# Retention with samples: small copies moved to GpSimd, and the last head's loads asked for in another order

## The chip, the cores and the metric

The kernel runs on one core of one Trainium2 chip. Its time is the device time of a whole execution in microseconds (us), the median of several runs. The core has a tensor engine (TensorE, in the profile PE for its matmuls and PEld for its weight loads), a vector engine (VectorE, DVE), a scalar engine (ScalarE, ACT), GpSimd (POOL), and SyncE (SP), which here only issues DMAs. Each engine works through its own list of instructions strictly in order. A DMA is issued by one of them, here mostly by SyncE and some by ScalarE, and an issue that has to wait holds up everything behind it on that engine.

## The reference

One inference step of a hybrid decoder: 1024 prompt tokens, and 8 sequences of 4 new tokens each (the samples, 32 rows). All is float32. The inputs, normalised, go through one wide projection; retention with 4 heads and latent attention (MLA) with 8 heads work beside each other on its parts; both are gated, projected, merged and projected again. The change is in the retention:

```python
def retention_chunk(q, k, v, s_prev, log_g):
    ...
    scores = jnp.einsum('bihd,bjhd->bhij', q, k) * dmask[None]
    intra = jnp.einsum('bhij,bjhe->bihe', scores, v)
    q_decay = jnp.exp((idx[:, None] + 1.0) * log_g[None, :])
    cross = jnp.einsum('bihd,bhde->bihe', q, s_prev) * q_decay[None, :, :, None]
    k_decay = jnp.exp((c - 1.0 - idx)[:, None] * log_g[None, :])
    s_new = (jnp.exp(c * log_g)[None, :, None, None] * s_prev
             + jnp.einsum('bjhd,bjhe->bhde', k * k_decay[None, :, :, None], v))
    return intra + cross, s_new
```

For the prompt this runs over 8 chunks of 128 tokens with the state (256 x 512 per head) carried along. For the samples it runs once, with a state of its own for each sequence that is read from memory (state_ret) and written back (ret_sample). q and k are rotated by tables of cosines and sines before.

## The kernel before, in words

A float32 matmul that must be exact is done as three: each operand is split into a high and a low part, and the products high x high, low x high and high x low are summed in PSUM. These are lines 268 to 270; one such group is called a triple here. A column block of a projection is 8 triples deep for each third (352 tokens) of the tokens; the thirds go through two PSUM banks, named mm. The gates' columns are emptied by ScalarE (L441, tile gev, two rooms) and stored by a DMA that ScalarE issues (L444).

The retention goes head by head. For a head, head_qk projects and rotates q and k (tables cosR and sinR; the last steps of a third are L848 to L853 on VectorE and GpSimd), and copies the samples' 32 columns into the small tiles qS and kS (L869). head_w loads and splits the weights of the values. prompt_chunks then takes the 8 chunks: front makes the scores and turns k (knl is read back from memory, where SyncE stored it, L951), values_of projects the values (vnh and vnl, two rooms each, L887 on ScalarE), and back updates the state S (first chunk L972 on ScalarE, later L970 on VectorE), splits it (Sth on GpSimd, Stl on VectorE), and makes the output, which is normalised (L894 to L906), turned on VectorE (tile g) and stored (go).

sample_state follows at the end of a head. It projects the values of the 32 rows with plain weights (wvS, eight blocks of 128x512, which use the rooms of vnh and vnl, four in all; matmuls L1090), copies them (vs, ScalarE, L1098), spreads them (L1101), and then takes four pieces of the state (st, two tiles of 512 KB each; calls of states): it multiplies them with q (L1122), adds k times v (L1136, VectorE L1138) and stores them (L1140).

These parts are Python generators. A function woven() interleaves two of them by their declared costs: the last chunk's remains and the samples of a head go beside the next head's projections, and for the last head beside three columns of the MLA gate. The written order is then rearranged once more by a scheduler that works with its own estimates of when a tile's room or data is ready. So the order on each engine is fixed when the program is built, and a load that seems ready earlier can draw the work that uses it forward. With the last head, the next phase's latents (lat, krT), rope weights (wr and wqr, rope_weights, L1156 and L1158) and projections' weights are asked for on SyncE's queue too.

A room is named by a tag: tiles with the same tag share rooms, and a new tile waits for the last reader of the room's old tile.

Of the kernel before, what the change touches and what calls it, by code (L numbers as in the profile page):

```python
# [10 lines left out]
F32 = mybir.dt.float32  # L11
# [9 lines left out]
P = 128  # L21
D = 1024
SEQ = 1024
# [3 lines left out]
NT = SEQ + NR  # L27
# [4 lines left out]
HR = 4  # L32
DK = 256
DV = 512
# [10 lines left out]
C_RQ, C_RK, C_RV, C_RG, C_LAT, C_MG, C_GA, C_GB = 0, 1024, 2048, 4096, 6144, 6848, 7872, 8896  # L45
# [117 lines left out]
def decode_step(ctx: ExitStack, tc: tile.TileContext, A: dict, O: dict):  # L163
    nc = tc.nc
    pe, act, dve, pool, sp = nc.tensor, nc.scalar, nc.vector, nc.gpsimd, nc.sync
# [18 lines left out]
    def ac():  # L184
        return banks["pool"].tile([P, 512], F32, tag="ac", name="ac", bufs=3)
# [3 lines left out]
    def slots(pl, tag, bufs):  # L189

        return lambda name, shape=(P, NT), dt=F32R: pl.tile(list(shape), dt, tag=tag, name=name, bufs=bufs)
# [35 lines left out]
    w_in = A["w_in"][0]  # L227
# [223 lines left out]
    def chain(*gs):  # L451
        for g_ in gs:
            yield from g_
# [355 lines left out]
    p4 = ph.enter_context(tc.tile_pool(name="p4", bufs=1))  # L809
# [5 lines left out]
    vs = p4.tile([P, DV], F32, name="vs")  # L815
    pool.memset(vs, 0.0)
    tok = slots(p4, "tok", 4)
    cosR, sinR = (p4.tile([P, NT], F32, name=n) for n in ("cosR", "sinR"))
    sp.dma_start(cosR, A["ropeR"][:, 0, :])
    sp.dma_start(sinR, A["ropeR"][:, 1, :])  # L820
    lg = _log_g()
# [4 lines left out]
    def head_qk(h, X):  # L826
        cols = [col + h * DK + m * P for col in (C_RQ, C_RK) for m in range(2)]
        ws = []

        def ask():  # L830
            if cols:
                col = cols.pop(0)
                ws.append(load_w(w_in[:, col:col + P], 8))

        ask()
        for name in "qk":
            dst = X[name] = [tok(f"{name}{m}", dt=F32) for m in range(2)]

            def first(j, ps, sl, dst=dst):
                act.copy(dst[0][:, sl], ps)  # L840

            def second(j, ps, sl, dst=dst, name=name):
                x = wst.tile([P, TH], F32, tag="gev", name="rx", bufs=2)
                act.copy(x, ps)
                c, s = cosR[:, sl], sinR[:, sl]
                x0, x1 = dst[0][:, sl], dst[1][:, sl]
                t = [p4.tile([P, TH], F32, tag=f"rt{i}", name=f"rt{i}", bufs=1) for i in range(2)]
                dve.tensor_tensor(out=t[0], in0=x0, in1=s, op=ALU.mult)  # L848
                dve.tensor_tensor(out=x1, in0=x, in1=c, op=ALU.mult)
                pool.tensor_tensor(out=x1, in0=x1, in1=t[0], op=ALU.add)  # L850
                dve.tensor_tensor(out=t[1], in0=x, in1=s, op=ALU.mult)
                dve.tensor_tensor(out=x0, in0=x0, in1=c, op=ALU.mult)
                pool.tensor_tensor(out=x0, in0=x0, in1=t[1], op=ALU.subtract)  # L853
                if name == "k":
                    n = min(TH, SEQ - j * TH)
                    bs = slice(j * TH // 32, (j * TH + n) // 32)
                    for m in range(2):
                        st = p4.tile([P, TH], F32, tag=f"rt{m}", name="kb", bufs=1)[:, :n].rearrange("p (b r) -> p b r", r=32)
                        dve.transpose(st, dst[m][:, j * TH:j * TH + n].rearrange("p (b r) -> p b r", r=32))
                        for a in range(0, P, 32):  # L860
                            sp.dma_start(kD[h % 2][bs, :, m * P + a:m * P + a + 32].rearrange("b i f -> i b f"), st[a:a + 32])
            for m, evac in enumerate((first, second)):
                for i, cost in enumerate(gemm(ws.pop(0), xn, evac, 8)):
                    if i == 3:
                        ask()
                    yield cost
            own = X[name + "S"] = p4.tile([P, 2, NR], F32, tag=name + "S", name=name + "S", bufs=2)
            for m in range(2):
                act.copy(own[:, m], dst[m][:, SEQ:])  # L869

    def head_w(h, X):

# [56 lines left out]
    def prompt_chunks(h, X):  # L929
        q, k = X["q"], X["k"]  # L930
# [69 lines left out]
        def ahead(u):  # L1000

            for cost in u:
                if cost is None:
                    return
                yield cost
# [6 lines left out]
        due, done = iter(()), 0.0  # L1012
        for c in range(8):
            if c == 7:
                X["st"] = [states(h, 0, 0)]
            u = back(c, parts)
            if c < 7:
                if c:
                    parts = front(c + 1)
                    yield 1.0  # L1020
                coming = values_of(c + 1, X, V)
                if c < 2:
                    yield from islice(coming, 3)
                both = woven((chain(due, ahead(u)), 3.5), (coming, 9.0))
                for cost in both:
                    yield cost
                    if c == 0:
                        done += cost
                        if done > 3.5:
                            parts, done = front(1), -99.0  # L1030
                            yield 1.0
                due = u
        yield None
        yield from due
        yield from ahead(u)
        X["st"].append(states(h, 0, 1))
        yield from u
        sp.dma_start(O["ret_prompt"][0, 0, h].rearrange("(m p) e -> p m e", p=P), S.rearrange("p (m e) -> p m e", m=2))

    def states(h, i, m):  # L1040

        pairs = []
        for half in range(2):
            if h + 1 == HR and i:
                st = tok("st", (P, 2, DV), F32)
            else:
                st = p4.tile([P, 2, DV], F32, tag="st", name="st", bufs=4)
            sp.dma_start(st, A["state_ret"][0].rearrange("(r i) h (m p) e -> i m h p r e", i=2, m=2)[i, m, h][:, 2 * half:2 * half + 2])
            pairs.append(st)
        return pairs  # L1050

    def sample_state(h, X):

        q, k = X["qS"], X["kS"]
        g4 = float(np.exp(NS * lg[h]))

        def weights(k):
            raw = p4.tile([P, DV], F32, tag="vn" + "hl"[k % 2], name="wvS", bufs=2)
            sp.dma_start(raw, w_in[k * P:(k + 1) * P, C_RV + h * DV:C_RV + (h + 1) * DV])
            return raw  # L1060

        raws_ = [weights(k) for k in range(4)]
        ks = p4.tile([P, 2, 4, 4, 8], F32, tag="knh", name="ks", bufs=2)
        for m in range(2):
            pool.tensor_copy(ks[:, m], k[:, m].rearrange("p (r x) -> p r x", x=8).unsqueeze(2).to_broadcast([P, 4, 4, 8]))
# [22 lines left out]
        for n in range(8):  # L1088
            for r in range(4):
                pe.matmul(ps[r * NR:(r + 1) * NR, :P], xS[:, n], raws_[n][:, r * P:(r + 1) * P], start=n == 0, stop=n == 7,  # L1090
                          tile_position=(0, r * NR), skip_group_check=True)
            if n < 4:
                raws_.append(weights(n + 4))
            if n == 3:
                yield 4.0
        for r in range(4):
# [21 lines left out]
        for n, (i, m) in enumerate(turns):  # L1118
            pairs = loaded.pop(0)
            st = [pairs[r // 2][:, r % 2, :] for r in range(4)]  # L1120
            for r in range(4):
                ins = pe.matmul(px[32 * r:32 * r + 32, :], qm[:, m, r, i], st[r], start=False, stop=n == 3,  # L1122
                                tile_position=(0, 32 * r), skip_group_check=True)
                if n > 1:
                    tc.keep_in_program_order(ins)
            if n == 3:
                on = group_norm(px, P, C("qdS", h, 1), C("qd2S", h, 1))
                if h + 1 < HR:
                    late.append((h, on, NS * 2, SEQ))
                else:  # L1130
                    turn_out(h, on, NS * 2, SEQ, (wst, "wl", 2))
                    store_out(sp)
            pd = [ac(), ac(), tr(), tr()]
            for r in range(4):
                rs = slice(32 * r, 32 * r + 32)
                pe.matmul(pd[r], kxs[i][rs, m * P:(m + 1) * P], vst[rs], start=True, stop=True, tile_position=(32 * r, 0))  # L1136
            for r in range(4):
                dve.scalar_tensor_tensor(out=st[r], in0=st[r], scalar=g4, in1=pd[r], op0=ALU.mult, op1=ALU.add)  # L1138
                if r % 2:
                    sp.dma_start(out[i, m, h][:, r - 1:r + 1], pairs[r // 2])  # L1140
            if n < 2:
                loaded.append(states(h, *turns[n + 2]))
            yield 3.8

# [20 lines left out]
    X, first_w = {}, []  # L1165
    run(head_in(0, X))
    for h in range(HR):
# [7 lines left out]
        else:  # L1175
            raws = [(qkA if i < 3 else qkB)("lat", (P, SEQ), F32) for i in range(5)]
# [12 lines left out]
        X = nxt  # L1189
# [245 lines left out]
    for h in range(HM):  # L1435
        ahead = prep(h + 1) if h + 1 < HM else iter(())
# [288 lines left out]
    raws = []  # L1725
# [110 lines left out]
```

## Time and profile before

| | us |
|---|---|
| timed runs: median (lowest to highest of three) | 2119.05 (2117.35 to 2122.88) |
| profiled execution: span | 2129.5 |
| TensorE busy in it | 2079.5 |
| VectorE, ScalarE, GpSimd busy | 1237.4, 692.8, 305.4 |

No time of the profiled execution other than its span is given; it is 10.5 us above the median of the timed runs. The retention lies from about 700 to 1330 us of that span. In the profile, a line that lists an instruction ends with the idle time of its engine before it, and with what ended that idle time. Matmuls overlap, so the start of one to the start of the next is their pace, not the duration. The list of waits of one engine gives the total, the number and the longest.

### The profile page before, as it was taken

What the parts mean: (1) busy time and instruction counts of PE and PEld (TensorE: products, weight loads), DVE (VectorE), ACT (ScalarE), POOL (GpSimd) and SP (SyncE); (2) the same over time, 40 slices, a digit from 0 to 9 for tenths busy, and PEclk for the clock granted to TensorE, in tenths of its full rate; (3) what the DMA queues carried; (4) which work ended last, traced back from release to release, by engine and by line L of the source; (5) the groups of instructions that cost most, each with busy time, mean ns of one, the idle gap of its engine ahead of it and who ended that gap; (6) DMA issues with size and microseconds to landing.
All of it is one profiled execution on the core that took longest, in us unless ns stands there. A gap on an engine that the chain in (4) does not pass through costs nothing. (4 is left out here: it accounts for less than half of the span.)

```text
span 2129.5 us, 38253 instructions
## 1 busy us (share of the span) xinstructions
PE 2079.5 (98%) x15122; PEld 1792.7 (84%) x15122; DVE 1237.4 (58%) x2699; ACT 692.8 (33%) x1455; POOL 305.4 (14%) x517
## 2 busy tenths in 40 slices
PE   8999999999999999999999999999999999999998
PEld 7898777777777897888878786788888999999976
DVE  6524555465655357667676663877777465454443
ACT  6312222433333222222222221454556232232221
POOL 2210110111110022222222120122211000000000
PEclk9999999999999999999999999999999999999999
DMA  7576656566565332554634746210112565236642
GB/s 211 129 241 211 234 186 237 187 244 216 211 228 178 111 94 51 175 163 120 204 67 151 191 134 221 64 49 18 38 52 92 187 217 173 89 122 132 172 153 91
DMA packets 387188, 321.90 MB, mean 151 GB/s; under 512 B 197984, under 2 KB 332320, under 8 KB 382912
## 3 DMA queue, kind: packets, MB, share of 16 engines
q1 hardware_dynamic: 290816, 205.86, 33.0%
q0 software_dynamic: 9216, 83.89, 10.5%
q10 hardware_dynamic: 86976, 29.70, 5.2%
q8 instruction: 119, 1.95, 0.4%
q14 instruction: 61, 0.50, 0.1%
HBM read 246.69 MB, written 72.69 MB: 150 GB/s over the span
## 5 line engine op out<-in xcount | busy, mean ns | idle before, releaser
L268 PE MATMUL mm<-xh,wh 128*128 128x352 f32 x1344 | 456.5, 340 | 4.8 <-ACT gev L441 3.2
L270 PE MATMUL mm<-xh,wl 128*128 128x352 f32 x1344 | 437.0, 325 | 2.1 <-DVE wl L200 2.1
L269 PE MATMUL mm<-xl,wh 128*128 128x352 f32 x1344 | 436.7, 325 | 0.0
L268 PEld LDWEIGHTS mm<-xh,wh 128*128 128x128 f32 x1344 | 253.7, 189 | 88.5 <-issue 76.8
L270 PEld LDWEIGHTS mm<-xh,wl 128*128 128x128 f32 x1344 | 254.6, 189 | 2.9 <-DVE wl L200 2.4
L269 PEld LDWEIGHTS mm<-xl,wh 128*128 128x128 f32 x1344 | 254.7, 189 | 2.5 <-issue 1.3
L691 DVE STREAM_TRANSPOSE kt<-craw 128x512 f32<-128x512 f32 x256 | 161.3, 681 | 108.8 <-PE sc L695 75.4
L200 DVE TENSOR_TENSOR wl<-wr,wh 128x512 fp32r<-128x512 f32 (+2 forms) x203 | 136.9, 686 | 98.7 <-ACT wh L249 69.1
L249 ACT CAST wh<-wr 128x512 fp32r<-128x512 f32 x150 | 89.8, 617 | 196.5 <-PE mm L269 169.8
L441 ACT ACTIVATE gev<-mm 128x352 f32<-128x352 f32 x120 | 55.5, 462 | 230.4 <-PE mm L270 221.8
L268 PE MATMUL mm<-mh,wh 128*128 128x352 f32 x384 | 124.8, 325 | 2.2 <-ACT mh L1210 0.8
L269 PE MATMUL mm<-ml,wh 128*128 128x352 f32 x384 | 124.7, 325 | 0.8 <-DVE ml L200 0.6
L270 PE MATMUL mm<-gh,wl 128*128 128x352 f32 x384 | 124.3, 324 | 0.0
L268 PE MATMUL mm<-gh,wh 128*128 128x352 f32 x384 | 124.3, 324 | 0.0
L270 PE MATMUL mm<-mh,wl 128*128 128x352 f32 x384 | 124.2, 324 | 0.0
L269 PE MATMUL mm<-gl,wh 128*128 128x352 f32 x384 | 124.1, 323 | 0.0
L268 PE MATMUL mm<-wv,xh 128*128 128x512 f32 x256 | 101.7, 397 | 0.0
L270 PE MATMUL mm<-wv,xl 128*128 128x512 f32 x256 | 100.9, 394 | 0.0
L269 PE MATMUL mm<-wv,xh 128*128 128x512 f32 x256 | 100.8, 394 | 0.0
L695 PE MATMUL sc<-kt,q 32*32 32x512 f32 x2560 | 91.2, 600 | 0.0
L268 PEld LDWEIGHTS mm<-mh,wh 128*128 128x128 f32 x384 | 72.4, 189 | 3.2 <-ACT gh L1210 1.2
L269 PEld LDWEIGHTS mm<-ml,wh 128*128 128x128 f32 x384 | 72.3, 188 | 1.6 <-DVE ml L200 1.4
(416 smaller groups left out, 4292.3 us busy)
## 6 DMA issues: line engine op xcount, KB each, us to landing
wr<-in_w_in_dram SPq DMA_DIRECT2D x144, 256.0 KB, 3.5
st<-in_state_ret_dram SPq DMA_DIRECT2D x32, 512.0 KB, 5.7
out_ret_sample_dram<-st SPq DMA_DIRECT2D x32, 512.0 KB, 3.1
gt<-gev ACTq DMA_DIRECT2D x48, 176.0 KB, 2.1
gl<-go SPq DMA_DIRECT2D x16, 528.0 KB, 5.1
rg<-gt SPq DMA_DIRECT2D x16, 528.0 KB, 4.2
gate<-ga SPq DMA_DIRECT2D x16, 528.0 KB, 3.6
wvS<-in_w_in_dram SPq DMA_DIRECT2D x32, 256.0 KB, 4.6
```

Of the source, the lines that this page charges most:

```text
L200: dve.tensor_tensor(out=out, in0=src, in1=b32(hi), op=ALU.subtract)
L249: hi_by[0](hi, raw)
L268: pe.matmul(out, wh, xh, start=first, stop=False)
L269: pe.matmul(out, wh, xl, start=False, stop=False)
L270: pe.matmul(out, wl, xh, start=False, stop=last)
L441: a = act.activation(t, ps, func)
L691: dve.transpose(kt[:, 2 * i + s].rearrange("p (n r) -> p n r", r=32), src)
L695: pe.matmul(sc[32 * v:32 * v + 32, q, :], Q["q4"][qs_, j + v // 2, 2 * (g % 2) + v % 2, :], kt[qs_, v, :], start=n == 0, stop=n == NJ // 2 ...
```

## The change

It has three parts. The samples' copies of q and k are made by GpSimd instead of ScalarE, for all four heads. In the last head, the value weights of the samples no longer all use the rooms of vnh and vnl: four of the eight go, two by two, into the rooms of the tables cosR and sinR, which no later head needs, and are asked for before the sixth chunk; two more are asked for after the last full chunk and two after the last chunk's matmuls. And the last two pieces of the state are asked for ahead of the last chunk's output stores, instead of within sample_state. For the last head the remains of the seventh chunk (its turn and store) come after the matmuls of the eighth.

```diff
-    cosR, sinR = (p4.tile([P, NT], F32, name=n) for n in ("cosR", "sinR"))
+    cosR, sinR = (p4.tile([P, NT], F32, tag=n, name=n) for n in ("cosR", "sinR"))
...
-                act.copy(own[:, m], dst[m][:, SEQ:])
+                pool.tensor_copy(own[:, m], dst[m][:, SEQ:])
...
+            if h + 1 == HR and c == 5:
+                X["raws"] = [raw for n in range(2) for raw in two_weights(h, 2 * n, ("cosR", "sinR")[n])]
             u = back(c, parts)
...
                 due = u
+        if h + 1 == HR:
+            X["raws"].extend(sample_weights(h, k) for k in (4, 5))
         yield None
-        yield from due
-        yield from ahead(u)
+        if h + 1 < HR:
+            yield from due
+            yield from ahead(u)
+        else:
+            yield from ahead(u)
+            X["raws"].extend(sample_weights(h, k) for k in (6, 7))
+            yield from due
         X["st"].append(states(h, 0, 1))
+        if h + 1 == HR:
+            X["st"].extend(states(h, 1, m) for m in range(2))
         yield from u
...
+    def sample_weights(h, k):
+        raw = p4.tile([P, DV], F32, tag="vn" + "hl"[k % 2], name="wvS", bufs=2)
+        sp.dma_start(raw, w_in[k * P:(k + 1) * P, C_RV + h * DV:C_RV + (h + 1) * DV])
+        return raw
+
+    def two_weights(h, k, tag):
+        raw = p4.tile([P, 2, DV], F32, tag=tag, name="wvS2")
+        sp.dma_start(raw, w_in[k * P:(k + 2) * P, C_RV + h * DV:C_RV + (h + 1) * DV].rearrange("(s p) e -> p s e", p=P))
+        return [raw[:, i, :] for i in range(2)]
...
-        raws_ = [weights(k) for k in range(4)]
+        raws_ = X["raws"] if h + 1 == HR else [sample_weights(h, k) for k in range(4)]
...
-            if n < 4:
-                raws_.append(weights(n + 4))
+            if len(raws_) < 8:
+                raws_.append(sample_weights(h, n + 4))
...
-            if n < 2:
+            if n < 2 and h + 1 < HR:
                 loaded.append(states(h, *turns[n + 2]))
```

The orders on three engines show what this moves. First SyncE's queue from the last head's latents on, before (st is a piece of the state, go the outputs, krT and lat the latents):

```order
L1048 DMA st<-in_state_ret_dram 128x2x512 x2
L1178 DMA lat<-latD 128x1024
L1181 DMA krT<-latD 64x1024 x2
L924 DMA go_105<-g 32x16x32 x4
L1048 DMA st<-in_state_ret_dram 128x2x512 x2
L924 DMA go_105<-g 32x16x32 x4
L1038 DMA out_ret_prompt_dram<-S 128x2x512
L1059 DMA wvS<-in_w_in_dram 128x512 x8
L1156 DMA wr<-in_w_uq_dram 128x4x64 x3
L1048 DMA st<-in_state_ret_dram 128x2x512 x2
```

and the same stretch in the changed kernel, where line numbers after the edit are higher by up to 15 (1059 is st there, 1065 wvS, 1155 the state's store, 1171 the rope weights):

```order
L1193 DMA lat<-latD 128x1024 x2
L1196 DMA krT<-latD 64x1024 x2
L1065 DMA wvS<-in_w_in_dram 128x512 x2
L924 DMA go_105<-g 32x16x32 x4
L1059 DMA st<-in_state_ret_dram 128x2x512 x4
L924 DMA go_105<-g 32x16x32 x4
L1049 DMA out_ret_prompt_dram<-S 128x2x512
L1155 DMA out_ret_sample_dram<-st 128x2x512 x2
L1171 DMA wr<-in_w_uq_dram 128x4x64 x3
L1155 DMA out_ret_sample_dram<-st 128x2x512 x2
```

The weights' last two stand ahead of both groups of output stores, the states between them, and the rope weights behind the first two stores of a state. The other six blocks are further up the queue: four of them, as two DMAs, around the last k's store, some rows after the tables' last use.

Second TensorE, at the samples of the last head, before:

```order
L270 MATMUL mm<-xh_127,wl 128x352
L1090 MATMUL ac<-wvS,xS 32x128 x32
L1101 MATMUL tr<-vs,turn 128x512
L1114 MATMUL ac<-vs,sms 128x512
L1122 MATMUL ac<-st,qm 32x512 x5
L1136 MATMUL ac<-vst,kx 128x512 x2
```

and now (gate triples stand at the dots: 8, 5, 4):

```order
L1105 MATMUL ac<-wvS_13290,xS 32x128 x8
L1105 MATMUL ac<-wvS_13292,xS 32x128 x8
...
L1105 MATMUL ac<-wvS,xS 32x128 x16
...
L1116 MATMUL tr<-vs,turn 128x512
...
L1129 MATMUL ac<-vs,sms 128x512
L1137 MATMUL ac<-st,qm 32x512 x4
L1151 MATMUL ac<-vst,kx 128x512 x2
```

Before, 40 gate triples stood ahead of the first of these and 24 behind; now 8 stand ahead of the first sixteen, 8 ahead of the next sixteen, and the others between the later steps.

Third GpSimd, at the last head's first chunk, before:

```order
L850 TENSOR_TENSOR k_12432<-k_12432,rt_12750 128x352
L900 TENSOR_TENSOR gr<-gv,cst 128x1
L853 TENSOR_TENSOR k_12431<-k_12431,rt_12751 128x352
L197 TENSOR_SCALAR Sth<-S 128x512 x4
```

and now:

```order
L850 TENSOR_TENSOR k_12432<-k_12432,rt_12750 128x352
L869 COPY kS<-k_12432 128x32
L900 TENSOR_TENSOR gr<-gv,cst 128x1
L853 TENSOR_TENSOR k_12431<-k_12431,rt_12751 128x352
L869 COPY kS<-k_12431 128x32
L197 TENSOR_SCALAR Sth<-S 128x512 x4
```

Each copy stands right behind the instruction that makes its input, and the second one ahead of the split of the state. On ScalarE the same copies are gone, and nothing else moved there until the gates' columns of the last head.

More of the change, by code (lines that the diff above doesn't have):

```diff
@@ L1055, in sample_state @@
         g4 = float(np.exp(NS * lg[h]))
[L1057 to L1060, printed above, removed]
-        raws_ = [weights(k) for k in range(4)]
+        raws_ = X["raws"] if h + 1 == HR else [sample_weights(h, k) for k in range(4)]
         ks = p4.tile([P, 2, 4, 4, 8], F32, tag="knh", name="ks", bufs=2)
```

## The prediction

> **What bounds the kernel now.** I read the busy table first, then the list of waits of TensorE, then the windows around the last retention head, and last the engines' instructions in order of time there.
>
> ```profile
> span 2129.5 us, 38253 instructions
> PE 2079.5 (98%) x15122; PEld 1792.7 (84%) x15122; DVE 1237.4 (58%) x2699; ACT 692.8 (33%) x1455; POOL 305.4 (14%) x517
> ```
>
> TensorE (PE) is busy for all but 2129.5 - 2079.5 = 50.0 us. The change adds and removes no matmul, so it can only win back waits of PE, and time in which PE counts as busy but runs below its pace. From PE's list of waits, the three that the change is about:
>
> ```profile
> PE ac L269 <- DVE vnl L200: 4.5, 7, 1.0
> PE ac L1090 <- DMA wvS<-in_w_in_dram: 3.5, 3, 2.1
> PE tr L1101 <- ACT vs L1098: 1.2, 1, 1.2
> ```
>
> The columns are the total in us, how often, and the longest. The last two are one place, the end of the last head. Windows there (length, then busy time of PE, PEld, DVE, ACT, POOL, the granted PE clock, the DMA share and GB/s):
>
> ```profile
> 1276.10:1296.30 20.20, 20.20 (x128) 19.97 (x125) 4.03 (x12) 4.02 (x8) 1.81 (x6) 1.00 0.77 213
> 1296.30:1312.90 16.60, 11.93 (x92) 3.85 (x91) 3.78 (x8) 2.97 (x9) 0.51 (x1) 0.69 0.62 193
> 1312.90:1330.30 17.40, 17.40 (x100) 12.91 (x98) 10.31 (x20) 1.60 (x3) 0.56 (x1) 1.00 0.71 264
> 1330.30:1340.00 9.70, 7.66 (x35) 6.32 (x34) 8.15 (x20) 6.89 (x15) 2.09 (x4) 0.82 0.44 107
> ```
>
> From 1296.3 to 1312.9 PE idles for 4.7 us, and its clock stands at 0.69 on average: the busy 11.9 us are slow ones. What runs there, PE in order of time (start, duration, line):
>
> ```profile
> 1276.70 0.41 PE L268 MATMUL mm<-xh,wh 128*128 128x352 f32 x1
> ...
> 1296.31 1.08 PE L1090 MATMUL ac<-wvS,xS 128*32 128x128 f32 x32
> 1299.46 0.43 PE L1090 MATMUL ac<-wvS,xS 128*32 128x128 f32 x8 [2.07 <-DMA wvS<-in_w_in_dram]
> ...
> 1301.96 1.30 PE L1090 MATMUL ac<-wvS,xS 128*32 128x128 f32 x16 [1.20 <-DMA wvS<-in_w_in_dram]
> 1304.44 2.08 PE L1101 MATMUL tr<-vs,turn 128*128 128x512 f32 x2 [1.18 <-ACT vs L1098]
> 1306.31 1.91 PE L1114 MATMUL ac<-vs,sms 128*128 128x512 f32 x2
> ...
> 1312.89 0.43 PE L268 MATMUL mm<-xh,wh 128*128 128x352 f32 x1
> ...
> 1322.50 1.06 PE L1122 MATMUL ac<-st,qm 128*32 128x512 f32 x8
> ...
> 1323.93 0.43 PE L268 MATMUL mm<-xh,wh 128*128 128x352 f32 x1
> ...
> 1331.81 0.36 PE L268 MATMUL ac<-wqr,lh 128*128 128x256 f32 x1 [1.31 <-ACT lh L1224]
> ```
>
> PE has used up 40 gate triples (L268 to L270) by 1296.31 and then has only the samples' chain, whose value weights (wvS) are not there: a DMA, PE, a ScalarE (ACT) copy, PE, one after the other with nothing between. The weights are late because of SyncE's queue:
>
> ```profile
> 1276.99 4.63 SPq L924 DMA_DIRECT2D go<-g  x4
> 1288.03 10.55 SPq L1059 DMA_DIRECT2D wvS<-in_w_in_dram  x8
> ```
>
> Their first DMA is issued at 1288.03, behind the output stores (go), and the eight take 10.55 us, since only four rooms exist.
>
> **The last head, part by part.** The order lists put the sixteen matmuls of the first four weights 8 gate triples after the start of this stretch, the other sixteen 8 later, and the rest of the chain with 5, 4, 9, 6, 2, 9 and 13 triples between its steps. The total is 64 triples in both kernels. So the price of the new stretch is its work at full pace. The pace comes from the head before, where the same chain ran among other matmuls:
>
> ```profile
> 1149.57 1.08 PE L1090 MATMUL ac<-wvS,xS 128*32 128x128 f32 x32
> 1150.58 0.43 PE L268 MATMUL mm<-xh,wh 128*128 128x352 f32 x1
> ...
> 1161.60 1.02 PE L1101 MATMUL tr<-vs,turn 128*128 128x512 f32 x2
> ...
> 1162.62 0.32 PE L269 MATMUL mm<-xl,wh 128*128 128x352 f32 x1
> ...
> 1164.88 1.02 PE L1114 MATMUL ac<-vs,sms 128*128 128x512 f32 x2
> ...
> 1167.54 0.32 PE L269 MATMUL mm<-xl,wh 128*128 128x352 f32 x1
> ```
>
> Gate triples: (1296.31 - 1276.70) / 40 = 0.490 us each, 64 of them 31.4. L1090: 1150.58 - 1149.57 = 1.01 for sixteen, 2.0 for both. L1101: up to the second matmul of the next triple, less one third of a triple, 1162.62 - 1161.60 - 0.16 = 0.9. L1114 with the first state: 1167.54 - 1164.88 - 0.16 = 2.5. The other three states: 1323.93 - 1322.50 = 1.43 each, 4.3. Sum 41.1 us. Today the stretch lasts from 1276.70 to the end of the gates, 1331.81 - 1.31 = 1330.50: 53.8 us. The difference is **12.7 us**. Of it 3.5 + 1.2 = 4.7 are waits; at most 0.31 x 16.6 = 5.1 is the clock; the rest is the state matmuls that today go one by one at VectorE's (DVE's) pace.
>
> Whether new waits eat it, step by step from 1276.70. The first four weights go into the tables of cosines and sines, asked for when those are dead, some 70 us ahead. The last pair is asked for after the final chunk's matmuls, ahead of the 4.63 us of stores, near 1273 instead of 1288. PE wants it at 1276.70 + 16 x 0.49 + 1.0 = 1285.5. What could delay it is the traffic:
>
> ```profile
> 1260.00:1270.00 10.00, 10.00 (x46) 8.00 (x45) 6.70 (x19) 1.55 (x3) 3.09 (x8) 1.00 0.98 305
> mg<-gev ACTq DMA_DIRECT2D x9, 176.0 KB, 4.3
> wr<-in_w_uq_dram SPq DMA_DIRECT2D x3, 128.0 KB, 4.4
> L1138 DVE SCALAR_TENSOR_TENSOR st<-st,ac 128x512 f32<-128x512 f32 x32 | 20.7, 675 | 7.0 <-PE tr L1136 6.4 <-PE ac L1136 0.6
> ```
>
> The DMA engines are full there. Four weights of 256 KB are added, 1 MB at 305 GB/s: 3.4 us more of queue, against some 8 us to spare. I put it at nothing; uncovered, each late us is one of PE. The copies vs have 5 triples (2.4 us) to hide in and took 1.2; DVE's state updates have 4 to 9 triples. One wait is new. The rope weights' loads (wr, L1156) now stand behind the first state's two output stores, which wait for DVE. ACT's casts of them (wqr) stand ahead of the copy that empties the gates' PSUM bank (gev), and PE has two such banks. The first state is through PE 25 triples (12.2) and 2.0 + 0.9 + 2.5 later than 1276.7, at 1294.3; four updates of 0.68 make it 1297, three issues 1298.5, and with 4.4 us to land (last row but one) the last cast can start near 1303. The bank is wanted after 15 more triples (7.3), one state (1.43) and a part of the next (0.5), at 1303.5. Price 0 to 2 us; I take 0.5, and 0.2 for seams. Asking for the last two states early costs two SyncE issues and no wait: PE wants them after 1304. So the term is **12.0**, with ends 7 (a 2 us wait, and a slow stretch of the clock at 3.5, between 0.18 x 9.7 = 1.7 and the 5.1 above) and 13.
>
> The gap at 1330.5 stays: after the last gate column ACT still has that copy and the first cast lh to do in this order. It costs 1.31 us and a clock of 0.82 over 9.7 us both before and after.
>
> The slow clock follows the idle: 0.69 after waits of 2.07 and 1.20, 0.82 after 1.31. The Trainium skill, "TensorE: Matmul & The Clock Gate", Part 1, says that the clock halves only after an idle window of about 3.4 us and returns after as long a busy one. The length of the slow stretch agrees; that it began after less idle does not, and the trace decides. By the page a new 1 us wait would cost 1 us alone, by the trace up to 3; that is in my lower end.
>
> **The head boundaries.** Sixteen small copies (L869, 128x32, four for each head) leave ACT. At the last of each head ACT stood waiting for GpSimd (POOL):
>
> ```profile
> 1213.37 0.22 ACT L869 COPY kS<-k 128x32 f32<-128x32 f32 x1 [6.07 <-POOL k L853]
> 1215.30 0.58 ACT L887 CAST vnh<-mm 128x512 fp32r<-128x512 f32 x1
> 1212.40 0.94 POOL L853 TENSOR_TENSOR k<-k,rt 128x352 f32<-128x352 f32 x1 [1.01 <-DVE rt L851]
> 1214.40 1.20 POOL L197 TENSOR_SCALAR Sth<-S 128x512 fp32r<-128x512 f32 x2 [1.06 <-ACT S L972]
> 1216.66 0.68 DVE L200 TENSOR_TENSOR vnl<-mm,vnh 128x512 fp32r<-128x512 f32 x1
> 1217.39 0.51 PE L269 MATMUL ac<-vnl,knh 128*128 128x512 f32 x1 [0.95 <-DVE vnl L200]
> L1065 POOL COPY ks<-kS x8: 284/289/293, 857.5 to 1263.4; 128x128 f32<-128x128 f32 x8
> ```
>
> ACT waits 6.07 us for k, then copies S, on which POOL waits (1214.40), on which DVE waits before it makes vnl, on which PE waits. Without the copy ACT does S while POOL is still at k. POOL then goes from k (ends 1212.40 + 0.94 = 1213.34) over its own copy to Sth. That copy isn't in the trace; ends are ACT's 0.22 and POOL's 0.29 for four times the elements; I take 0.29. Sth starts at 1213.63 instead of 1214.40, 0.77 earlier, and vnl can follow, since vnh is there at 1215.88. The same picture stands at three boundaries: **2.1** after 0.2 off for the first head, where POOL did not wait for ACT. Ends: -1 (each copy on the path, nothing gained) and 4.5 (all seven waits). The Trainium skill, "SBUF — State Buffer", section "Who interferes with whom", speaks against this edit: GpSimd and a VectorE operation with two SBUF inputs exclude each other for a whole instruction. By it the copies could give back what they win, this term 0 and the sum 12.0. The copy stands beside transposes with one input at the boundary, so I keep the row's value.
>
> **Sum.** 12.0 + 2.1 = 14.1 us off the profiled execution: 2129.5 to 2115.4. The median of the timed runs is 2119.05, 10.5 below that span; I take the gain over unchanged: **2105 us**. Less than 0.3% (6.4 us) this measurement cannot tell from no change.
>
> **The rivals.**
> *The chain waits again (wqr).* The rope loads land late, the gates' bank isn't emptied, PE stops for 2 us, the clock falls as it did after 1.31 us. For: ACT works strictly in order, and loads stand behind stores that wait for DVE. Against: the bank leaves 3.9 us per column third. Gain 12.7 - 2 - 3.5 = 7 at the last head and 0 to 2 at the boundaries: 2110 to 2112.
> *The change doesn't do what it says.* If the last weight pair is as late as before, because its rooms (vn) are released late or the full DMA engines serve it last, the first sixteen matmuls alone move and PE runs out of triples again: only the 2 to 4 us of one wait are won, 2115 to 2120.
> *Slower: the stores of the gates.* Three MB (weights and the two states) now move in a stretch at 0.98 DMA share. A gate third can only start when the store of the one before the last has landed: 4.3 us now against 7.8 available (16 triples). Seven thirds remain. To cancel 14.1 us each must be 2.0 late, which is a landing of 7.8 + 4 = 12 us; from 14 us on, the kernel is slower by more than 0.3%. That would be 2126 or more. Against it: 3 MB at 305 GB/s are 10 us spread over 70.
>
> **How the numbers follow.** Forecast (2101 to 2108) 0.63; the wqr wait 0.18; not what it says 0.14; the stores 0.05. Faster by over 0.3% is the forecast, and nearly all of the wqr wait: 0.80. Within 0.3% 0.16, slower 0.04. The range runs from 13 + 4.5 off, 2101, to the far side of the wqr wait, 2113.
>
> **What would show it.** Right: no wait for wvS or vs at PE, the clock at 1.00 from the last chunk to the end of the gates, the wvS matmuls among gate triples, that stretch near 42 us, and waits for vnl at three boundaries of a few tenths. Wrong: a wait for gev or for st in that stretch, a clock below 1.00 there, or waits for vnl unchanged with Sth no earlier after k. The forecast fails most likely by the bank behind wqr.

## The result

The changed kernel takes 2110.08 us (median of 8 runs, 2106.96 to 2114.45) where the kernel before took 2120.97 us on the same chip (8 runs, 2117.35 to 2126.10). The ratio is 0.9948, 95% interval 0.9938 to 0.9958: 10.9 us faster (9 to 13), where 14.1 was forecast. Measured again on another chip later (after_again, below), the ratio was 0.9924, 0.9910 to 0.9937: 16 us (13 to 19). The gain forecast lies between the two. Of the times, 2110.08 us is inside the range given (2101 to 2113), but in the part that the prediction kept for its rival wqr (2110 to 2112) and not in the forecast's own (2101 to 2108); the traces below show that this rival did not happen. That the second time, 2105.40, is nearly the 2105 forecast is luck in part, since the kernel before had 2123.05 beside it and not 2119.05.

The head of the profile after, and its two rows of TensorE's waits that belong to the change (total, how often, longest):

```profile
span 2106.9 us, 38261 instructions
PE 2067.5 (98%) x15122; PEld 1788.6 (85%) x15122; DVE 1237.4 (59%) x2699; ACT 690.9 (33%) x1439; POOL 309.8 (15%) x533
```

```profile
PE ac L269 <- DVE vnl L200: 4.2, 7, 1.2
...
PE ac L268 <- ACT lh L1239: 1.5, 1, 1.5
```

The waits for wvS, vs and vnh are gone. The wait for vnl is nearly as long as before (4.5). Two more rows of the kernel before matter below; vnh is waited for at three head boundaries, ll behind the gates:

```profile
PE ac L268 <- ACT vnh L887: 1.0, 3, 0.3
...
PE ac L270 <- DVE ll L200: 0.7, 1, 0.7
```

Sixteen instructions have moved from ScalarE (1455 to 1439) to GpSimd (517 to 533). The span is 22.6 us shorter than in the profile before, twice the timed gain; the experiments before_again and before_third show where most of the rest arises.

The last head in the changed kernel, in windows (length, then busy time of PE, PEld, DVE, ACT, POOL, the granted PE clock, the DMA share and GB/s). The first three rows go from its first gate triple to the last, the fourth is the rotation of the queries behind them:

```profile
1264.70:1284.90 20.20, 20.20 (x171) 17.05 (x171) 7.65 (x18) 4.63 (x12) 1.82 (x6) 1.00 0.91 266
1284.90:1301.50 16.60, 16.60 (x108) 12.35 (x107) 7.51 (x15) 2.51 (x6) 0.52 (x1) 1.00 0.79 266
1301.50:1307.10 5.60, 5.60 (x35) 5.32 (x33) 3.06 (x9) 1.13 (x2) 0.56 (x1) 1.00 0.62 223
1308.60:1318.30 9.70, 9.68 (x59) 8.45 (x59) 9.32 (x25) 6.66 (x14) 0.49 (x2) 1.00 0.31 101
```

TensorE is busy throughout and the clock is 1.00, where the kernel before had 11.93 us of work in 16.60 at a clock of 0.69. In order of time, TensorE there (start, duration, line):

```profile
1264.76 0.41 PE L268 MATMUL mm<-xh,wh 128*128 128x352 f32 x1
...
1268.83 1.08 PE L1105 MATMUL ac<-wvS,xS 128*32 128x128 f32 x32
1273.90 1.08 PE L1105 MATMUL ac<-wvS,xS 128*32 128x128 f32 x32
1277.44 1.02 PE L1116 MATMUL tr<-vs,turn 128*128 128x512 f32 x2
1280.24 1.02 PE L1129 MATMUL ac<-vs,sms 128*128 128x512 f32 x2
1281.19 1.07 PE L1137 MATMUL ac<-st,qm 128*32 128x512 f32 x8
1287.20 1.06 PE L1137 MATMUL ac<-st,qm 128*32 128x512 f32 x8
1293.56 1.06 PE L1137 MATMUL ac<-st,qm 128*32 128x512 f32 x8
1299.11 1.07 PE L1137 MATMUL ac<-st,qm 128*32 128x512 f32 x8
1308.62 0.38 PE L268 MATMUL ac<-wqr,lh 128*128 128x256 f32 x1 [1.51 <-ACT lh L1239]
```

The profile counts two records for each of the plain matmuls, so x32 at L1105 is sixteen of them. No row of the chain has an idle time behind it until the last. From 1264.76 to the end of the gates, 1308.62 - 1.51 = 1307.11, are 42.4 us; the kernel before needed 53.8 and the forecast was 41.1 + 0.7. What was asked for when, on SyncE's queue and then on ScalarE:

```profile
1264.13 1.84 SPq L1065 DMA_DIRECT2D wvS<-in_w_in_dram  x2
1266.07 5.42 SPq L924 DMA_DIRECT2D go<-g  x4
...
1285.69 2.04 SPq L1171 DMA_DIRECT2D wr<-in_w_uq_dram  x3
```

```profile
1288.79 0.93 ACT L1173 CAST wqr<-wr 128x256 fp32r<-128x256 f32 x2 [8.38 <-DMA wr<-in_w_uq_dram]
1290.15 0.41 ACT L1173 CAST wqr<-wr 128x256 fp32r<-128x256 f32 x1 [0.43 <-DMA wr<-in_w_uq_dram]
1290.46 0.46 ACT L441 ACTIVATE gev<-mm 128x352 f32<-128x352 f32 x1
```

The last pair of weights goes out ahead of the output stores (go) and is there when TensorE wants it at 1273.90. ScalarE does wait 8.38 us for the rope weights, and gev stands behind the casts, as the prediction feared; but the bank is emptied in time.

One head boundary in the changed kernel (ScalarE, GpSimd, VectorE and TensorE, in order of time):

```profile
1197.97 0.57 ACT L887 CAST vnh<-mm 128x512 fp32r<-128x512 f32 x1
...
1201.22 0.95 POOL L853 TENSOR_TENSOR k<-k,rt 128x352 f32<-128x352 f32 x1 [1.01 <-DVE rt L851]
...
1202.23 0.21 POOL L869 COPY kS<-k 128x32 f32<-128x32 f32 x1
...
1202.45 1.21 POOL L197 TENSOR_SCALAR Sth<-S 128x512 fp32r<-128x512 f32 x2
...
1203.11 1.09 DVE L200 TENSOR_TENSOR Stl<-S,Sth 128x512 fp32r<-128x512 f32 x1
...
1204.72 0.68 DVE L200 TENSOR_TENSOR vnl<-mm,vnh 128x512 fp32r<-128x512 f32 x1
...
1205.45 0.50 PE L269 MATMUL ac<-vnl,knh 128*128 128x512 f32 x1 [0.80 <-DVE vnl L200]
```

ScalarE no longer waits for k and has vnh ready 6 us before VectorE uses it for vnl. GpSimd goes from k over its own copy (0.21 us; ScalarE's took 0.22) straight to Sth, 0.28 us behind k instead of 1.06. TensorE still waits 0.80 us, because VectorE makes Stl, which waits for Sth, ahead of vnl.

### The profile page after: what moved, and what is told of

It is laid out like the page before. It is cut to its first block, busy times and chain, and to the rows that moved or that the text cites. A ratio compares the mean times of both kernels' runs of the same rounds, so it can differ in the third digit from the quotient of the medians.

```text
span 2106.9 us, 38261 instructions
## 1 busy us (share of the span) xinstructions
PE 2067.5 (98%) x15122; PEld 1788.6 (85%) x15122; DVE 1237.4 (59%) x2699; ACT 690.9 (33%) x1439; POOL 309.8 (15%) x533
## 3 DMA queue, kind: packets, MB, share of 16 engines
q0 software_dynamic: 9216, 83.89, 10.7%
```

## The experiments

All times of sections below are read in the same way. Four marks are taken from rows like these of the kernel before in its third profile (before_third) and of the changed kernel in its second (after_again): the first x matmul of L784 (the end of the paged attention), the first and the last transposes tr<-qS of the samples' queries (of the first and of the last head), and the first rotation matmul ac<-wqr,lh. After the colon stand minimum, median and maximum in ns, then first and last start in us:

```profile
L784 PE MATMUL x<-out,wv x32: 190/276/402, 716.7 to 720.4; 128*128 128x32 f32 x32
L1076 PE MATMUL tr<-qS,ks x16: 194/276/276, 862.5 to 1266.0; 128*128 128x32 f32 x16
L268 PE MATMUL ac<-wqr,lh x24: 277/280/356, 1319.7 to 1342.2; 128*128 128x256 f32 x24
```

```profile
L784 PE MATMUL x<-out,wv x32: 190/276/276, 715.9 to 719.3; 128*128 128x32 f32 x32
L1091 PE MATMUL tr<-qS,ks x16: 194/276/276, 860.1 to 1261.4; 128*128 128x32 f32 x16
L268 PE MATMUL ac<-wqr,lh x24: 277/280/385, 1305.4 to 1328.2; 128*128 128x256 f32 x24
```

The distances between the marks, in us, for every profile. "Three heads" is from the first tr<-qS to the last, "last head" from there to the first rotation matmul, "rotation" from the first to the last of the 24:

| profile | paged attention ends | to first head | three heads | last head | rotation | span |
|---|---|---|---|---|---|---|
| before | 728.6 | 144.1 | 403.9 | 55.2 | 24.0 | 2129.5 |
| before_again | 729.1 | 144.2 | 405.4 | 55.0 | 23.9 | 2132.4 |
| before_third | 716.7 | 145.8 | 403.5 | 53.7 | 22.5 | 2117.7 |
| copies_only | 728.2 | 144.2 | 401.3 | 54.6 | 24.1 | 2127.0 |
| loads_only | 724.0 | 144.2 | 403.6 | 44.0 | 22.9 | 2114.6 |
| weights_late | 728.1 | 144.1 | 401.8 | 54.9 | 24.0 | 2126.7 |
| pair_late | 725.7 | 144.2 | 401.7 | 45.6 | 22.8 | 2112.9 |
| states_late | 727.4 | 144.1 | 403.0 | 44.0 | 22.9 | 2116.1 |
| due_first | 727.7 | 144.1 | 401.7 | 44.9 | 22.9 | 2115.3 |
| after | 718.2 | 144.1 | 402.3 | 44.0 | 22.9 | 2106.9 |
| after_again | 715.9 | 144.2 | 401.3 | 44.0 | 22.8 | 2103.3 |
| split_act | 726.2 | 142.9 | 402.3 | 44.0 | 22.9 | 2114.5 |
| split_act_again | 716.6 | 142.9 | 401.1 | 44.0 | 22.9 | 2102.5 |
| split_above | 720.8 | 146.0 | 401.1 | 44.0 | 22.8 | 2110.0 |

**copies_only: the kernel before with the samples' copies on GpSimd, nothing else.**

```
-                act.copy(own[:, m], dst[m][:, SEQ:])
+                pool.tensor_copy(own[:, m], dst[m][:, SEQ:])
```

> The kernel before with one edit: GpSimd makes the samples' copies. Theory (two separate gains, nearly all of it at the last head): the last head's stretch, from the first gate triple after the samples' first small matmuls to the end of the gates, stays at 53.8 us as before; the waits of TensorE for vnh and vnl at the head boundaries fall from 5.5 us to 4.2 as in the changed kernel; the time is 1 to 2 us below before, ratio 0.999 to 1.000. Rival (the copies free ScalarE for the gates too, and are worth a large part of the 11 us): the stretch shrinks by 3 us or more and the ratio is below 0.998.

**loads_only: the changed kernel with these copies back on ScalarE.**

```
-                pool.tensor_copy(own[:, m], dst[m][:, SEQ:])
+                act.copy(own[:, m], dst[m][:, SEQ:])
```

> The changed kernel with the samples' copies back on ScalarE. Theory: the last head's stretch is 42.4 us as in the changed kernel, TensorE's waits at the boundaries are 5.5 us as before, the time is 9 to 12 us below before (ratio 0.9945 to 0.996). Rival: the stretch is longer than 45 us, and the ratio above 0.997.

Timed, copies_only is no different from the kernel before (2129.42 against 2128.55 us, ratio 1.0001, 0.9990 to 1.0012), and loads_only is faster (2119.61 us, ratio 0.9963, 0.9949 to 0.9977). In the traces each part does its own thing and no other. One head from tr<-qS to tr<-qS, of the kernel before, of copies_only and of loads_only:

```profile
872.70:1007.70 135.00, 133.52 (x752) 111.90 (x751) 91.06 (x197) 33.80 (x72) 34.00 (x59) 1.00 0.51 144
```

```profile
872.40:1006.70 134.30, 133.34 (x752) 111.89 (x751) 91.16 (x197) 33.24 (x68) 35.00 (x63) 1.00 0.52 145
```

```profile
868.20:1003.30 135.10, 133.59 (x752) 111.96 (x751) 91.28 (x198) 33.96 (x72) 34.37 (x59) 1.00 0.52 144
```

The copies take 0.7 to 0.8 us off this head. Over the three heads, the mean of the four profiles with ScalarE's copies is 404.1 us, and of the seven with GpSimd's, split_act and its two relatives left aside, 401.9: 2.2 us. The early loads take the last head from 55 to 44.0 us whether or not the copies move. Two parts in two places, which add up; but the 2.2 us of copies_only do not show in its time, whose interval reaches from 2.1 us faster to 2.6 us slower.

**weights_late: the changed kernel with all eight weights of the last head asked for in sample_state, as before.** The early states and the new order of the last chunk's remains are kept.

```
-            if h + 1 == HR and c == 5:
-                X["raws"] = [raw for n in range(2) for raw in two_weights(...)]
...
-            X["raws"].extend(sample_weights(h, k) for k in (4, 5))
...
-            X["raws"].extend(sample_weights(h, k) for k in (6, 7))
...
-        raws_ = X["raws"] if h + 1 == HR else [sample_weights(h, k) for k in range(4)]
+        raws_ = [sample_weights(h, k) for k in range(4)]
```

> The changed kernel with all eight value weights of the last head asked for within the samples' part again, in the four old rooms; the early states and the order of the chunk's remains stay as in the change. Theory (the weights' place decides, since with it the scheduler spreads the gate triples): the stretch is 52 to 55 us, with TensorE waits for wvS of 3 us or more and a clock of 0.65 to 0.75 in the slow part. Rival (the early states or the order of the remains carry a good part): the stretch is below 50 us.

**pair_late: the changed kernel with only the last pair asked for late.** In this kernel the late pair loads blocks 4 and 5 a second time in place of 6 and 7, so the last head's sample values are made from other data of the same size; the work and the traffic are the same.

```
-            X["raws"].extend(sample_weights(h, k) for k in (6, 7))
```

> The changed kernel with only the last pair of weights asked for within the samples' part. The order on TensorE then has 8 triples, 16 small matmuls, 8 triples, 8 small ones, 24 triples in one go, and after them the chain with hardly a triple between its steps. Theory A (the spread of the gate triples is what wins, the wait for the weights is the smaller part): the weights are there in time, no wait for wvS, but the chain waits for ScalarE and VectorE, and the stretch is 46 to 49 us with a clock below 1.00 in it; time 4 to 8 us below before. Theory B (the wait for the weights and the clock after it are the whole loss): no wait for wvS and a stretch of 42 to 44 us. Third case (the pair is late): a wait for wvS of over 1 us and a stretch over 50 us.

TensorE's waits from 1260 us on, first of weights_late, then of pair_late:

```profile
PE ac L1100 <- DMA wvS<-in_w_in_dram: 3.6, 4, 2.7
...
PE tr L1111 <- ACT vs L1108: 1.2, 1, 1.2
```

```profile
PE tr L1115 <- ACT vs L1112: 1.2, 1, 1.2
```

weights_late is the kernel before again: the last head takes 54.9 us, TensorE takes 40 gate triples ahead of the chain, and the time is 2128.53 us (one run) where the kernel before had 2128.55. pair_late has no wait for wvS and needs 45.6 us (timed ratio 0.9951, 0.9935 to 0.9966), although its order has 24 triples in one block ahead of the last weights and almost none behind them, and the wait for vs stays. So of the 10.9 us between weights_late and the changed kernel, 9.3 come with six of the eight weights being early, and with them the clock; the last pair and the spreading of the triples that goes with it are worth 1.6. The expectation that the spreading itself carries much of the gain (46 to 49 us) missed.

**states_late: the changed kernel with the last two states asked for as before.**

```
-        if h + 1 == HR:
-            X["st"].extend(states(h, 1, m) for m in range(2))
...
-            if n < 2 and h + 1 < HR:
+            if n < 2:
```

> The changed kernel, but the last two states are asked for as before, one by one behind the stores of the first two states. Theory A (asking early buys nothing, since TensorE reaches them late enough): the stretch from the last transposes of the samples' queries to the first matmul of the query rotation stays at 44.0 us within 0.3, no wait for st. Theory B (the loads behind stores that wait for VectorE come too late): a wait for VectorE's st or for the bank tr of 1 to 3 us in it, 45 to 48 us in all.

**due_first: the changed kernel with the work due from the chunk before ahead of the last pair, so that the output stores are ahead of it in SyncE's queue.**

```
-        if h + 1 < HR:
-            yield from due
-            yield from ahead(u)
-        else:
-            yield from ahead(u)
+        yield from due
+        yield from ahead(u)
+        if h + 1 == HR:
             X["raws"].extend(sample_weights(h, k) for k in (6, 7))
-            yield from due
```

> The changed kernel, but the work due from the chunk before the last comes first again, so that its output stores stand in SyncE's queue ahead of the last pair of weights. Theory A (the pair must be ahead of the output stores): the pair is issued some 5 us later, the second sixteen weight matmuls wait 1 to 3 us for wvS, and the stretch grows from 44.0 to 45 to 48 us. Theory B (there is enough slack, 8 triples and more, because the order of the work moves with it): no wait for wvS, 44.0 us within 0.5.

states_late and due_first ran once each, so only their sections are read. states_late: 44.0 us, no wait for a state in the last head. Asking for these states early buys nothing here. due_first: 44.9 us and no wait for wvS. Its order of the work moves with it: TensorE takes the second sixteen weight matmuls in three pieces (8, 4 and 4) between triples, and does not wait among them, so the 0.9 us is lost in these seams, as far as the trace shows, and not in waiting. So the last pair has slack, and putting it ahead of the stores is worth under 1 us.

**before_again and before_third: the kernel before, profiled twice more.**

> The kernel before once more, unchanged, for a second profile. Theory A (the 8 to 10 us by which the profile of the changed kernel is ahead before the retention begins, up to the end of the paged attention, differ from execution to execution): the paged attention of this profile ends at another time than 718 or 728.6 us or at one of them by chance, while the last head's stretch is 55.2 us within 0.5 again, with waits of 3.5 for wvS and 1.2 for vs. Theory B (the change moves something there too): the paged attention ends at 728 to 729 us again.

> The kernel before a third time. In the traces so far TensorE either waits some 10 times (3.3 to 4.1 us) for ScalarE's pr in the paged attention, which then ends at 724 to 729 us, or never, and it ends at 716 to 721 us; the kernel split_act showed both, in two executions. Theory A (it goes by chip and execution, not by kernel): this profile may show either; if it shows none, the paged attention ends near 716 to 721 us, and span is near 2121. Theory B (the change takes these waits away somehow): the waits are there again, 728 to 729 us. The other sections stay: 403.9 to 405.4 for the three boundaries' heads, 55 for the last head's stretch.

The first profile of the changed kernel is 10.4 us ahead where the paged attention ends (718.2 against 728.6), in code that the change does not touch. What goes with it stands in TensorE's waits up to there; this row is from before_again:

```profile
PE x L720 <- ACT pr L711: 3.7, 9, 0.8
```

Nine profiles have it, with 7 to 9 waits, and end the paged attention at 724 to 729 us. Five have none, and end it at 716 to 721 us; before_third is one of these, and split_act shows both in its two profiles. It goes by chip or execution and not by kernel. These waits add up to 3.3 to 4.1 us, so they mark the longer executions and are not the whole difference; where the rest comes from stays open. Like with like, before_third against after_again: 2117.7 - 2103.3 = 14.4 us, of which 9.7 in the last head, 2.2 in the three heads, 1.6 on the way to the first head, 0.8 up to the end of the paged attention, and 0.1 behind the last head. The 1.6 is not the change's. Right behind the paged attention TensorE's clock was halved for 3.4 us in before_third, which costs up to 1.7 us, and for 6.8 us in split_above, the one other profile with 146 us there:

```profile
719.77:723.18 3.41, 3.41 (x15) 3.41 (x15) 1.02 (x2) 0.00 (x0) 2.13 (x8) 0.50 0.29 46
```

Why it was halved there, where TensorE had been busy, was not found.

**after_again, and a version that aims at the vnl waits that are left.** split_act gives the split of the first chunk's state to ScalarE, which is free at the boundary now; split_act_again is the same kernel, measured beside the changed one. split_above moves, on top of it, the copy into the table above behind the first split of the latents, since a releaser "DVE above" stands at ScalarE's first cast lh.

```
-                    hi_pool(Sh[:, vs], S[:, vs])
+                    (hi_pool if c else act.copy)(Sh[:, vs], S[:, vs])
```

```
-    dve.tensor_copy(above[:, 3 * P:], C("causal"))
...
     run(split_latents(range(3), ((0, 256), (256, 512), (512, SEQ))))
+    dve.tensor_copy(above[:, 3 * P:], C("causal"))
```

> The changed kernel with one line more: the first chunk's state S is split into its high part by ScalarE instead of GpSimd (later chunks as before). Theory A (what is left at the head boundaries, waits of 0.80 us for vnl at three and 1.2 at the first, comes from GpSimd making Sth only behind k, with VectorE's Stl ahead of vnl): the waits for vnl fall from 4.2 us in all to about 1, the three boundaries get 0.8 us shorter each, and the time falls by 2 to 3 us against the changed kernel, ratio to before near 0.9935. Theory B (ScalarE is in order: two more casts of 0.57 us delay its cast of vnh and its copies of other PSUM banks): vnl waits stay at 3 to 4 us or vnh waits come back, and the time is that of the changed kernel, ratio 0.995, or 1 to 2 us longer.

> The changed kernel once more, on one chip with the kernel before. From the sections of the traces so far the change takes 2.3 us at the head boundaries, 11.1 in the last head's stretch and 1.1 in the rotation behind it, 14.5 in all. Theory A (that is all of it): ratio to before 0.9932 within 0.001. Theory B (the first ratio, 0.9948, is right and 3 to 4 us are given back somewhere): 0.994 to 0.996 again, and a section of this profile that is longer than in the kernel before.

> The same kernel as split_act, beside the changed kernel on one chip. Its trace gave 1.2 us in the first head and nothing at the other three boundaries, so the two should differ by 1 us, less than 0.1%: ratio to before 0.0005 under that of after_again, not to be told apart. If ScalarE's split is worth the 3.6 us that the two separate measurements differed by, 0.0017 under it.

> split_act, and the copy of the causal block into the table above stands behind the first split of the latents instead of ahead of it. Theory A (ScalarE's first cast lh waits for that copy, as the wait of 0.55 us in the trace says): lh starts some 0.5 us earlier, TensorE's wait at the end of the gates falls from 1.5 to 1.0 us, and the rest of the time stays. Theory B (the name of the releaser is inferred, and it is the room of the closed pool that lh waits for): the wait stays at 1.5 us. In time 0.5 us can't be told.

| kernel | us | ratio to before, 95% interval |
|---|---|---|
| split_act (another chip) | 2114.70 | 0.9931, 0.9917 to 0.9945 |
| after_again | 2105.40 | 0.9924, 0.9910 to 0.9937 |
| split_act_again | 2104.27 | 0.9913, 0.9900 to 0.9927 |
| split_above | 2105.34 | 0.9912, 0.9899 to 0.9926 |

The last three stood beside the kernel before at 2123.05 us. split_act does what it should to the list of waits:

```profile
PE ac L269 <- DVE vnl L200: 1.5, 3, 0.5
```

The first head gains 1.2 us (142.9 against 144.1). But the three other heads take 402.3 and 401.1 us, as in the changed kernel: the order of the matmuls moved with the edit, and what the wait lost, busy time took up (133.63 us busy of 134.30 in one head, against 133.42 of 134.40 in after_again). A shorter wait in the list is no gain until the distance between two marks shrinks. In time split_act_again and after_again can't be told apart. In split_above the wait for lh stays at 1.5 us: the copy into above is not what holds it. What does was not found.

## Why the prediction was right, and where it was not

**The last head, 12.0 us.** Measured 11.4 between the two profiles of the prediction (53.8 to 42.4), and 9.7 to 11.2 by the marks, since the kernel before itself varies from 53.7 to 55.2 while the changed one is at 44.0 each time. The step "work at full pace" gave 41.1 + 0.7 and the chip 42.4, all of it work. That these agree to 0.6 us is luck in part: a gate triple took (1273.90 - 1268.83 - 1.01) / 8 = 0.508 us between the two groups of weights, and 33.0 / 64 = 0.515 over all, where the forecast took the 0.490 of an unbroken run of 40. That is 1.6 us more over 64, the other steps took 0.3 less, and of the 0.7 kept in reserve the 0.5 for a wait was not needed. The cause held: weights_late brings the whole loss back, states_late nothing.

**The price of the wqr wait, 0.5 us.** Not there. The casts came when the working said: the last one ends 1290.15 + 0.41 - 1264.76 = 25.8 us into the stretch, the forecast had it start 26 us in, and that was early enough. The rival that rested on it falls, and so does the one that the last pair comes too late: it was issued only 0.6 us ahead of the stretch, not 3.7, and still TensorE did not wait.

**The gap behind the gates, "stays".** The wait did (1.51 us, 1.31 before); its slow clock did not. The rotation takes 22.9 us where four profiles with the old loads took 24.0. This 1.1 us was missing from the sum. The five profiles with the old loads lost it four times, the nine with early loads never; but before_third, with the old loads and the same waits, has 22.5, so the old loads alone do not cost it. Behind the wait for lh the kernel before has a second one for ll, 0.73 us long, which is gone with the early loads except in pair_late; the last section shows what the two together do to the clock.

**The head boundaries, 2.1 us.** Measured 2.2 in the three heads and nothing in the first, by the mechanism forecast: Sth 0.78 us earlier behind k (0.28 against 1.06), and TensorE takes vnl 1205.45 - 1202.17 = 3.28 us behind the end of k instead of 1217.39 - 1213.34 = 4.05. The copies of k on this path took 0.21 us instead of 0.29. But the sign named for it, waits for vnl of a few tenths, failed: 0.80 is left of 0.95. The prediction did not count that TensorE also waited for vnh just ahead, 0.34 us at each of the three boundaries; that wait went as well, so TensorE comes to vnl earlier. The Trainium skill, "SBUF — State Buffer", section "Who interferes with whom", would have made this term 0, if the copies had blocked VectorE; VectorE's busy time in the head above is 91.06 us with ScalarE's copies and 91.16 with GpSimd's, so no such loss is seen here. Beside one another the two engines do hold each other up, as these rows of the changed kernel show:

```profile
885.78 1.15 POOL L850 TENSOR_TENSOR q<-q,rt 128x352 f32<-128x352 f32 x1 [3.44 <-DVE q L849]
886.05 1.43 DVE L200 TENSOR_TENSOR wl<-wr,wh 128x512 fp32r<-128x512 f32 x1
886.99 0.56 POOL L869 COPY qS<-q 128x32 f32<-128x32 f32 x1
```

wl, of two inputs, takes 0.69 us in the median of its 40 and 1.43 here, beside GpSimd's L850; the copy of q, 0.21 us where nothing of that kind runs, takes 0.56 and ends 0.07 us behind wl. This happens to one copy of q in each head, and nothing waits for it.

**The stores of the gates.** The DMA share is 0.91 with 266 GB/s in the first 20 us of the stretch, and TensorE waits for none of it. The gates' stores landed in 3.5 us in the median and 6.4 at most, against the 7.8 that were available. That rival falls too.

**The sum and the time.** The sections give 2.2 + 10.7 + 0 to 1.1, 13 to 14 us (10.7 is the mean of 55.2, 55.0, 53.7, 54.6 and 54.9, less 44.0), against 14.1 forecast; from before_third alone, which lost less clock in the last head and behind it (halved for 6.8 us, for 10.2 to 13.7 in the other four), they give 2.2 + 9.7 - 0.3 = 11.6. Timed it was 10.9 (9 to 13) on one chip and 16 (13 to 19) on the other. Why the two differ stays open: they are pairs of medians a tenth of a percent uncertain, and one section outside the change swings by 10 us between executions. On the chip of loads_only the same doubt shows: 7.9 us timed (5 to 11), where its last head and its rotation are 12 us shorter than in the first profile of the kernel before. The timed executions leave no sections to compare.

## What to carry to other kernels

Price a stretch that has run out of filler by its own work at the pace of an undisturbed neighbour, not by the waits listed in it: here 4.7 us of waits stood for some 11 us, because the clock and the one-by-one order came with them. Get the loads ahead of the queue first, and spread the order second: six early weights gave 9.3 us, the last pair and the spreading 1.6. Before a difference of two profiles is put down to a change, compare the sections that the change cannot reach, and measure distances between fixed marks rather than sums of waits.

## What was not expected of the hardware

The granted clock is 1.00 or 0.50 in these profiles, and it changes on a grid of 3.41 us that lies elsewhere in each execution. Windows on that grid, first in the kernel before, at the weights and then at the waits for lh and ll:

```profile
1296.64:1300.05 3.41, 1.18 (x36) 0.64 (x28) 0.00 (x0) 0.00 (x0) 0.00 (x0) 1.00 0.60 183
1300.05:1310.29 10.24, 7.80 (x37) 2.34 (x38) 2.44 (x5) 2.97 (x9) 0.51 (x1) 0.50 0.79 250
1330.77:1334.18 3.41, 1.64 (x12) 1.47 (x12) 3.11 (x8) 3.26 (x9) 1.81 (x4) 1.00 0.68 128
1334.18:1337.59 3.41, 3.41 (x11) 2.73 (x10) 3.36 (x9) 1.31 (x3) 0.00 (x0) 0.50 0.49 171
```

The same places in before_third, the same kernel:

```profile
1286.39:1289.80 3.41, 0.96 (x28) 0.42 (x24) 0.00 (x0) 0.00 (x0) 0.00 (x0) 1.00 0.71 212
1289.80:1296.63 6.83, 4.65 (x28) 1.62 (x26) 1.50 (x4) 2.97 (x9) 0.00 (x0) 0.50 0.85 265
1317.11:1320.52 3.41, 1.98 (x12) 1.51 (x11) 1.89 (x4) 2.06 (x6) 2.09 (x4) 1.00 0.72 118
1320.52:1323.93 3.41, 2.81 (x16) 2.50 (x17) 3.41 (x10) 2.86 (x6) 0.00 (x0) 1.00 0.82 270
```

The halved stretches in these rows last 10.24, 3.41 and 6.83 us, which is three, one and two times 3.41, and the two of the kernel before start 34.13 us apart, ten times 3.41. Around the last head, over all fourteen profiles, each of the nine windows of the grid at full clock in which TensorE was busy for half of it or less was followed by a halved one, and none of the eight with a share of 0.53 to 0.58 was. Half is no sharp threshold: elsewhere in these profiles windows of 0.53 were followed by a halved clock, one of 0.49 was not, and the halving at 719.77 in before_third followed a busy one.

So the averages of 0.69 and 0.82 that the prediction read are mixtures of 1.00 and 0.50, and a wait has no fixed price in clock: here it mattered how much of one window the waits together left idle, and so where they fell. The waits for lh and ll, 1.31 and 0.73 us, lie almost whole in one window in the kernel before, which was busy for 1.64 us, and are shared between two in before_third, busy for 1.98 and 2.81. In the changed kernel the one wait of 1.51 us is left there; an estimate from these numbers is that it leaves a window at least 3.41 - 1.51 = 1.90 us busy wherever it falls, a share of 0.56, which would keep the clock at 1.00. No run moved the grid or the waits to test this.

The Trainium skill, "TensorE: Matmul & The Clock Gate", Part 1, describes a window of some 3.4 us that runs freely, whatever the kernel does; the grid of 3.41 us, placed differently in each execution, agrees with that. That the clock was halved behind a window in which TensorE was busy for 1.64 of 3.41 us does not agree with the page's one idle window.
